# ReLU and row mean on one core: 127 rows a partition, the last 128 rows stored apart, and the tail shared between the engines

## The chip, the core and the metric

The kernel runs on one core of a Trainium2 chip. The metric is the device time of one execution in microseconds (us), the median of several runs. The profile is of one such execution; its span is some 1.8 us shorter than the measured time. Where two kernels are compared by a ratio, it is the mean time of one kernel's fast runs over that of the other's of the same rounds, so it is not quite the ratio of the medians that are quoted.

## The reference

```python
batch, seq, dim = 32, 512, 1024
x = np.random.randn(batch, seq, dim).astype(np.float32)      # 67.11 MB
relu_x = np.maximum(x, 0)
return np.mean(relu_x, axis=-1).astype(np.float32)           # 32 x 512 = 16,384 means, 65,536 B
```

Every number of x is read once and used once. The output is a thousandth of the input.

## The kernel before

The 16,384 rows are dealt to 128 partitions, 128 consecutive rows to each. A tile holds 16 rows of every partition (8 MB); seven full tiles come by one load each, the last one in pieces that get smaller, so that little work is left when the last byte lands. ScalarE and VectorE take the rows in turn; each makes the ReLU and the row's sum in one call (the trace shows it as two records, the pass over the row and a short read of the accumulated sum).

```python
    J = R // P                                               # 128 rows a partition
    xr = xf.rearrange("(p j) d -> p j d", p=P, j=J)
    outr = out.flatten().rearrange("(p j) -> p j", p=P, j=J)
    # ... seven tiles of 16 rows; the last tile in pieces of 8, 4, 2, 1 rows, its row 15 in 512, 256, 256 columns
    finish(0, j0)                                            # scale the sums of the first 112 rows
    # ... rows 0 to 13 of the last tile
    finish(j0, j0 + lo)

    last = xt[:, NB - 1, :]
    act_row(nc, xt[:, lo, :D // 2], part_a[:, 0:1])          # row 14, halved
    dve_row(nc, xt[:, lo, D // 2:], part_v[:, 0:1])
    act_row(nc, last[:, :D // 4], part_a[:, 1:2])            # row 15, four quarters
    dve_row(nc, last[:, D // 4:D // 2], part_v[:, 1:2])
    nc.vector.tensor_scalar(out=res[:, J - 2:J - 1], in0=part_a[:, 0:1], scalar1=part_v[:, 0:1], scalar2=inv,
                            op0=ALU.add, op1=ALU.mult)                                          # L106
    dve_row(nc, last[:, D // 2:3 * D // 4], part_v[:, 2:3])
    nc.vector.tensor_scalar(out=part_v[:, 1:2], in0=part_v[:, 1:2], scalar1=part_a[:, 1:2], scalar2=part_v[:, 2:3],
                            op0=ALU.add, op1=ALU.add)                                           # L111
    dve_row(nc, last[:, 3 * D // 4:], part_v[:, 3:4])
    nc.vector.tensor_scalar(out=res[:, J - 1:J], in0=part_v[:, 3:4], scalar1=part_v[:, 1:2], scalar2=inv,
                            op0=ALU.add, op1=ALU.mult)                                          # L116
    nc.sync.dma_start(out=outr, in_=res)                     # one store: 128 pieces of 512 B
```

## Time and profile before

| what | value | where it is read |
|---|---|---|
| time | 164.94 us (164.87 to 165.21, 4 runs) | runs |
| span of the profile | 163.1 us | page |
| last load landed | 159.19 us | landing records of the trace |
| last VectorE result | 160.61 us | timeline: 160.39 + 0.21 |
| store: issued, landed | 160.67, 162.22 us | timeline, landing records |

The page of the kernel before; the lines are the span, the busy time of the engines, the chain of work that ended last, and the store (KB, and us from issue to landing):

```profile
span 163.1 us, 351 instructions
DVE 75.4 (46%) x139; ACT 69.4 (43%) x133; POOL 0.2 (0%) x4
...
HBM read 67.11 MB, written 0.07 MB: 412 GB/s over the span
DMA 83%; DVE 14%; SPq 1%; issue 0%; DVEq 0%
...
out_dram<-res SPq DMA_DIRECT2D x1, 64.0 KB, 1.6
```

The kernel is bound by its loads: 83% of the chain is DMA, and the engines are busy less than half the time. Of the 896 packets of 65,536 B, the median took 2.418 us, which is 27.1 GB/s on each of 16 DMA engines, 434 GB/s in all. The Trainium skill ("DMA: Bandwidth & Descriptors", Specifications) gives the ceiling of the fabric as 435 GB/s, and the trace agrees. So a change can win only what lies after the last landing: 163.1 - 159.19 = 3.9 us.

The timeline of the kernel before, after the one-row piece has landed (start, us, engine, line, operation):

```profile
157.88 0.17 DVE L73 TENSOR_SCALAR res<-sum_v 128x7 f32<-128x7 f32 x1
...
157.96 0.68 DVE L20 TENSOR_SCALAR_CACHE_REDUCE xt<-xt 128x512 f32<-128x512 f32 x1
...
158.75 0.21 DVE L106 TENSOR_SCALAR res<-part_a,part_v 128x1 f32<-128x1 f32 x1
...
159.22 0.42 DVE L20 TENSOR_SCALAR_CACHE_REDUCE xt<-xt 128x256 f32<-128x256 f32 x1
159.56 0.08 DVE L20 DVE_READ_ACCUMULATOR xt<-xt 128x1 f32 x1
159.75 0.27 DVE L111 TENSOR_SCALAR part_v<-part_v,part_a 128x1 f32<-128x1 f32 x1
159.94 0.41 DVE L20 TENSOR_SCALAR_CACHE_REDUCE xt<-xt 128x256 f32<-128x256 f32 x1
160.27 0.08 DVE L20 DVE_READ_ACCUMULATOR xt<-xt 128x1 f32 x1
160.39 0.21 DVE L116 TENSOR_SCALAR res<-part_v 128x1 f32<-128x1 f32 x1
160.67 0.35 SPq L120 DMA_DIRECT2D out_dram<-res  x1
```

VectorE is late: the last 256 columns landed at 159.19 and their sum starts at 159.94. The small operations of lines 73, 106 and 111 are what made it late; those of lines 106 and 111 also wait some 0.1 us for the result just before them (159.56 + 0.08 to 159.75).

### The profile page before, as it was taken

What the parts mean: (1) busy time and instruction counts of PE and PEld (TensorE: products, weight loads), DVE (VectorE), ACT (ScalarE), POOL (GpSimd) and SP (SyncE); (2) the same over time, 40 slices, a digit from 0 to 9 for tenths busy, and PEclk for the clock granted to TensorE, in tenths of its full rate; (3) what the DMA queues carried; (4) which work ended last, traced back from release to release, by engine and by line L of the source; (5) the groups of instructions that cost most, each with busy time, mean ns of one, the idle gap of its engine ahead of it and who ended that gap; (6) DMA issues with size and microseconds to landing.
All of it is one profiled execution on the core that took longest, in us unless ns stands there. A gap on an engine that the chain in (4) does not pass through costs nothing.

```text
span 163.1 us, 351 instructions
## 1 busy us (share of the span) xinstructions
DVE 75.4 (46%) x139; ACT 69.4 (43%) x133; POOL 0.2 (0%) x4
## 2 busy tenths in 40 slices
DVE  0000039900596008940099202990059700799993
ACT  3000039700594008920099002980059500797890
POOL 0000000000000000000000000000000000000000
DMA  7979989989998998997997998998998897999970
GB/s 257 482 321 482 482 354 450 514 354 418 514 418 354 514 418 354 514 482 305 498 484 340 466 498 354 434 514 370 402 514 386 386 514 338 434 442 394 409 298 16
DMA packets 2162, 67.19 MB, mean 412 GB/s; under 512 B 240, under 2 KB 624, under 8 KB 880
## 3 DMA queue, kind: packets, MB, share of 16 engines
q1 hardware_dynamic: 2160, 67.18, 96.0%
q14 instruction: 2, 0.02, 0.0%
HBM read 67.11 MB, written 0.07 MB: 412 GB/s over the span
## 4 chain that ended last, share of the span: by engine, by line
DMA 83%; DVE 14%; SPq 1%; issue 0%; DVEq 0%
DMA xt<-in_x_dram 83%; DVE xt L20 13%; SPq L86 0%; SPq L79 0%; DVE part_v L111 0%; DVE res L116 0%; DVE res L106 0%; DVE res L73 0%; DVEq L20 0%; DVEq L111 0%; DVEq L106 0%
## 5 line engine op out<-in xcount | busy, mean ns | idle before, releaser
L20 DVE TENSOR_SCALAR_CACHE_REDUCE xt<-xt 128x1024 f32<-128x1024 f32 (+1 forms) x67 | 74.4, 1172 | 84.9 <-DMA xt<-in_x_dram 84.8
L15 ACT ACTIVATE xt<-xt 128x1024 f32<-128x1024 f32 (+1 forms) x65 | 66.7, 1027 | 88.9 <-DMA xt<-in_x_dram 88.9
L15 ACT ACTIVATION_READ_ACCUMULATOR xt<-xt 128x1 f32 x65 | 12.1, 187 | 0.0
L20 DVE DVE_READ_ACCUMULATOR xt<-xt 128x1 f32 x67 | 5.6, 83 | 0.0
L15 ACT ACT_TABLE_LOAD x1 | 1.3, 1283 | 0.7 <-PEq L135 0.7
L74 ACT ACTIVATE res<-sum_a 128x56 f32<-128x56 f32 (+1 forms) x2 | 0.5, 232 | 0.1
L73 DVE TENSOR_SCALAR res<-sum_v 128x56 f32<-128x56 f32 (+1 forms) x2 | 0.4, 184 | 0.1
L111 DVE TENSOR_SCALAR part_v<-part_v,part_a 128x1 f32<-128x1 f32 x1 | 0.3, 273 | 0.1
L106 DVE TENSOR_SCALAR res<-part_a,part_v 128x1 f32<-128x1 f32 x1 | 0.2, 214 | 0.1
L116 DVE TENSOR_SCALAR res<-part_v 128x1 f32<-128x1 f32 x1 | 0.2, 214 | 0.0
L135 POOL MEMSET const-uint8-127<- 128x1 uint8 x1 | 0.1, 102 | 0.0
L135 POOL MEMSET const-bfloat16-1.0<- 128x1 bf16 x1 | 0.1, 101 | 0.0
L135 POOL MEMSET const-float32-0.0<- 128x1 f32 x1 | 0.1, 98 | 0.2 <-issue 0.2
L135 POOL MEMSET const-float32-1.0<- 128x1 f32 x1 | 0.1, 98 | 0.0
## 6 DMA issues: line engine op xcount, KB each, us to landing
xt<-in_x_dram SPq DMA_DIRECT2D x1, 4096.0 KB, 39.0
xt<-in_x_dram SPq DMA_DIRECT2D x1, 2048.0 KB, 43.5
xt<-in_x_dram SPq DMA_DIRECT2D x1, 1024.0 KB, 45.5
xt<-in_x_dram SPq DMA_DIRECT2D x1, 512.0 KB, 46.3
xt<-in_x_dram SPq DMA_DIRECT2D x1, 256.0 KB, 46.5
xt<-in_x_dram SPq DMA_DIRECT2D x2, 128.0 KB, 42.7
xt<-in_x_dram SPq DMA_DIRECT2D x7, 48.9
out_dram<-res SPq DMA_DIRECT2D x1, 64.0 KB, 1.6
```

The lines of the kernel that those rows point to most:

```text
L15: nc.scalar.activation(out=src, in_=src, func=RELU, accum_out=acc)
L20: nc.vector.tensor_scalar(out=src, in0=src, scalar1=0.0, scalar2=None, op0=ALU.max, op1=ALU.add, accum_out=acc,)
L73: nc.vector.tensor_scalar_mul(out=res[:, lo + 1:hi:2], in0=sum_v[:, lo + 1:hi:2], scalar1=inv)
L74: nc.scalar.mul(out=res[:, lo:hi:2], in_=sum_a[:, lo:hi:2], mul=inv)
L106: nc.vector.tensor_scalar(out=res[:, J - 2:J - 1], in0=part_a[:, 0:1], scalar1=part_v[:, 0:1], scalar2=inv, op0=ALU.add, op1=ALU.mult,)
L111: nc.vector.tensor_scalar(out=part_v[:, 1:2], in0=part_v[:, 1:2], scalar1=part_a[:, 1:2], scalar2=part_v[:, 2:3], op0=ALU.add, op1=ALU.add,)
L116: nc.vector.tensor_scalar(out=res[:, J - 1:J], in0=part_v[:, 3:4], scalar1=part_v[:, 1:2], scalar2=inv, op0=ALU.add, op1=ALU.mult,)
L135: nc = _bacc.Bacc("TRN2", target_bir_lowering=False, num_devices=1)
```

## The change

Its intent: take the small operations off VectorE (GpSimd does the scaling), share the last row more evenly, and send nearly the whole output while the last row is still being summed. For that the last row of each partition must not lie between the others in memory, so each partition gets 127 rows, and the last 128 rows go one to a partition. What is left to store at the end is one value a partition, 128 x 4 B, side by side in memory.

```diff
-    xr = xf.rearrange("(p j) d -> p j d", p=P, j=J)
-    outr = out.flatten().rearrange("(p j) -> p j", p=P, j=J)
+    xr = xf[:P * (J - 1), :].rearrange("(p j) d -> p j d", p=P, j=J - 1)
+    outr = outf[:P * (J - 1)].rearrange("(p j) -> p j", p=P, j=J - 1)
+    xlast = xf[P * (J - 1):, :]
+    outlast = outf[P * (J - 1):].rearrange("(p o) -> p o", o=1)
 # ... finish(): one nc.gpsimd.tensor_scalar instead of one operation each on VectorE and ScalarE
+    act_row(nc, prev[:, :512], part[:, 0:1])
+    dve_row(nc, prev[:, 512:], part[:, 1:2])
+    nc.gpsimd.tensor_scalar(
+        out=res[:, J - 2:J - 1], in0=part[:, 0:1], scalar1=part[:, 1:2], scalar2=inv, op0=ALU.add, op1=ALU.mult,
+    )
+    nc.sync.dma_start(out=outr, in_=res[:, :J - 1])          # 128 pieces of 508 B, early
+    act_row(nc, last[:, :256], part[:, 2:3])
+    dve_row(nc, last[:, 256:512], part[:, 3:4])
+    nc.gpsimd.tensor_scalar(
+        out=part[:, 4:5], in0=part[:, 2:3], scalar1=inv, scalar2=0.0, op0=ALU.mult, op1=ALU.add,
+    )
+    act_row(nc, last[:, 512:640], part[:, 5:6])
+    dve_row(nc, last[:, 640:768], part[:, 6:7], init=part[:, 3:4])     # the sum starts from another
+    nc.scalar.activation(
+        out=part[:, 7:8], in_=part[:, 5:6], func=ACT.Identity, scale=inv, bias=part[:, 4:5],
+    )
+    dve_row(nc, last[:, 768:], part[:, 8:9], init=part[:, 6:7])
+    nc.vector.scalar_tensor_tensor(
+        out=end, in0=part[:, 8:9], scalar=inv, in1=part[:, 7:8], op0=ALU.mult, op1=ALU.add,
+    )
-    nc.sync.dma_start(out=outr, in_=res)
+    nc.sync.dma_start(out=outlast, in_=end)                  # 128 pieces of 4 B
```

The tail of before, shown above, goes. Called "after" from here on.

More of the change, by code (lines that the diff above doesn't have):

```diff
@@ L9, with dve_row @@
 ALU = mybir.AluOpType
-RELU = mybir.ActivationFunctionType.Relu
+ACT = mybir.ActivationFunctionType
 def act_row(nc, src, acc):
-    nc.scalar.activation(out=src, in_=src, func=RELU, accum_out=acc)
-def dve_row(nc, src, acc):
+    nc.scalar.activation(out=src, in_=src, func=ACT.Relu, accum_out=acc)
+def dve_row(nc, src, acc, init=None):
     nc.vector.tensor_scalar(
-        out=src, in0=src, scalar1=0.0, scalar2=None,
+        out=src, in0=src, scalar1=0.0, scalar2=init,
         op0=ALU.max, op1=ALU.add, accum_out=acc,
@@ L39 @@
     inv = 1.0 / D
-    xr = xf.rearrange("(p j) d -> p j d", p=P, j=J)
-    outr = out.flatten().rearrange("(p j) -> p j", p=P, j=J)
+    outf = out.flatten()
+    xr = xf[:P * (J - 1), :].rearrange("(p j) d -> p j d", p=P, j=J - 1)
+    outr = outf[:P * (J - 1)].rearrange("(p j) -> p j", p=P, j=J - 1)
+    xlast = xf[P * (J - 1):, :]
+    outlast = outf[P * (J - 1):].rearrange("(p o) -> p o", o=1)
     NB = 16
-    BUFS = 3
     full = J // NB - 1
-    row_pieces = []
-    left = NB
-    while left > 1:
-        row_pieces.append(left // 2)
-        left -= left // 2
-    col_pieces = [D // 2, D // 4, D // 4]
-    in_pool = ctx.enter_context(tc.tile_pool(name="in", bufs=BUFS))
+    row_pieces = [8, 4, 2, 1]
+    assert sum(row_pieces) == NB - 1
+    col_pieces = [512, 256, 256]
+    assert sum(col_pieces) == D
+    in_pool = ctx.enter_context(tc.tile_pool(name="in", bufs=3))
     res_pool = ctx.enter_context(tc.tile_pool(name="res", bufs=1))
-    sum_a = res_pool.tile([P, J], F32)
-    sum_v = res_pool.tile([P, J], F32)
+    sums = res_pool.tile([P, J], F32)
     res = res_pool.tile([P, J], F32)
-    part_a = res_pool.tile([P, 2], F32)
-    part_v = res_pool.tile([P, 4], F32)
+    part = res_pool.tile([P, 10], F32)
+    end = res_pool.tile([P, 1], F32)
     def rows(xt, lo, n, j0):
@@ L65, in rows @@
             j = j0 + k
-            if j % 2:
-                dve_row(nc, xt[:, k, :], sum_v[:, j:j + 1])
-            else:
-                act_row(nc, xt[:, k, :], sum_a[:, j:j + 1])
+            (dve_row if j % 2 else act_row)(nc, xt[:, k, :], sums[:, j:j + 1])
     def finish(lo, hi):
-        nc.vector.tensor_scalar_mul(out=res[:, lo + 1:hi:2], in0=sum_v[:, lo + 1:hi:2], scalar1=inv)
-        nc.scalar.mul(out=res[:, lo:hi:2], in_=sum_a[:, lo:hi:2], mul=inv)
+        nc.gpsimd.tensor_scalar(
+            out=res[:, lo:hi], in0=sums[:, lo:hi], scalar1=inv, scalar2=0.0, op0=ALU.mult, op1=ALU.add,
+        )
     for t in range(full):
@@ L83 @@
     xt = in_pool.tile([P, NB, D], F32, name="xt")
+    prev, last = xt[:, NB - 2, :], xt[:, NB - 1, :]
     lo = 0
@@ L89 @@
     for w in col_pieces:
-        nc.sync.dma_start(out=xt[:, lo, c:c + w], in_=xr[:, j0 + lo, c:c + w])
+        nc.sync.dma_start(out=last[:, c:c + w], in_=xlast[:, c:c + w])
         c += w
@@ L98 @@
     finish(j0, j0 + lo)
-    last = xt[:, NB - 1, :]
-    act_row(nc, xt[:, lo, :D // 2], part_a[:, 0:1])
-    dve_row(nc, xt[:, lo, D // 2:], part_v[:, 0:1])
-    act_row(nc, last[:, :D // 4], part_a[:, 1:2])
-    dve_row(nc, last[:, D // 4:D // 2], part_v[:, 1:2])
-    nc.vector.tensor_scalar(
-        out=res[:, J - 2:J - 1], in0=part_a[:, 0:1], scalar1=part_v[:, 0:1], scalar2=inv,
-        op0=ALU.add, op1=ALU.mult,
-    )
-    dve_row(nc, last[:, D // 2:3 * D // 4], part_v[:, 2:3])
-    nc.vector.tensor_scalar(
-        out=part_v[:, 1:2], in0=part_v[:, 1:2], scalar1=part_a[:, 1:2], scalar2=part_v[:, 2:3],
-        op0=ALU.add, op1=ALU.add,
-    )
-    dve_row(nc, last[:, 3 * D // 4:], part_v[:, 3:4])
-    nc.vector.tensor_scalar(
-        out=res[:, J - 1:J], in0=part_v[:, 3:4], scalar1=part_v[:, 1:2], scalar2=inv,
-        op0=ALU.add, op1=ALU.mult,
-    )
-    nc.sync.dma_start(out=outr, in_=res)
+    act_row(nc, prev[:, :512], part[:, 0:1])
+    dve_row(nc, prev[:, 512:], part[:, 1:2])
+    nc.gpsimd.tensor_scalar(
+        out=res[:, J - 2:J - 1], in0=part[:, 0:1], scalar1=part[:, 1:2], scalar2=inv, op0=ALU.add, op1=ALU.mult,
+    )
+    nc.sync.dma_start(out=outr, in_=res[:, :J - 1])
+    act_row(nc, last[:, :256], part[:, 2:3])
+    dve_row(nc, last[:, 256:512], part[:, 3:4])
+    nc.gpsimd.tensor_scalar(
+        out=part[:, 4:5], in0=part[:, 2:3], scalar1=inv, scalar2=0.0, op0=ALU.mult, op1=ALU.add,
+    )
+    act_row(nc, last[:, 512:640], part[:, 5:6])
+    dve_row(nc, last[:, 640:768], part[:, 6:7], init=part[:, 3:4])
+    nc.scalar.activation(
+        out=part[:, 7:8], in_=part[:, 5:6], func=ACT.Identity, scale=inv, bias=part[:, 4:5],
+    )
+    dve_row(nc, last[:, 768:], part[:, 8:9], init=part[:, 6:7])
[3 more added lines that the diff above has]
+    nc.sync.dma_start(out=outlast, in_=end)
 _INS = ['x']
```

## The prediction

> **What bounds the kernel now.** The load stream. The page's chain of work that ended last is 83% DMA, and the span is 163.1 us for 67.11 MB read. The packet records show 65,536 B packets at a constant 2.418 us from the second one on: 27.1 GB/s an engine, 434 GB/s on 16. The Trainium skill ("DMA: Bandwidth & Descriptors", Specifications) gives a fabric ceiling of 435 GB/s; this trace agrees, so the stream can't get faster. First packet 1.74 us, last load landing 159.19 us. VectorE needs 9.2 us for a tile of 16 rows against 19.4 us of transfer. Only what lies after the last landing, about 3.9 us of span, can be won.
>
> **The tail before (timeline of the last 8 us, and landings).** The one-row piece lands at 157.89, the column pieces at 158.53, 158.87 and 159.19. VectorE runs without a real gap from 156.62: two small scalings and joins (174, 214, 273 ns, each with about 0.1 us wait for its own previous result) stand between the row sums, so that the last 256 columns start at 159.94, 0.75 us after they landed. The last join ends at 160.61, the store is issued at 160.67, its first packet moves at 161.52, it lands at 162.22; closing barriers take the span to 163.1.
>
> **What the change does.**
> - Removes from VectorE the 174 ns scaling, the 214 and 273 ns joins and their waits, and 128 of 768 columns of the last row; about 0.9 us.
> - Adds: two sums that start from the previous one's result, so each waits for it (about 0.12 us) and reads a pointer operand (about 60 ns by 214 against 174 and 273 ns). About 0.35 us back, all on the chain. My chain: half row 157.9 to 158.55, 256 columns to 158.97, 128 to 159.4, 256 to 160.0, final join 160.15 to 160.4.
> - GpSimd has no arithmetic in the trace of before, so its op time is unknown. The join of partials before ScalarE's closing op must finish by about 159.8. [...] At 1 us an op it becomes the chain, and the end comes at about 161.2.
> - The large store (64 KB, 1.6 us) goes out near 159.2 to 159.6, hidden. The final store is 512 B as 128 pieces of 4 B. The 64 KB store needed 0.85 us to its first packet, 0.35 us of packets, 0.35 us to land; I expect 0.1 to 0.2 us saved.
> - Row pitch a partition goes from 512 to 508 KiB. The Trainium skill (same page, "Latency and other measured facts") has power-of-two pitches slowing copies, at 512 KiB by 3%. This trace shows 512 KiB already at the ceiling, so I expect nothing, at most 0.3 us in the first packets (2.7 to 3.5 us against 2.418).
>
> **Sum.** Final join 0.2 us earlier, store 0.1 us shorter: span about 162.8, time 164.6 us. A tail of no cost would gain little over 2%, so "within 2%".
>
> **Right if:** 65,536 B packets stay at 2.418 us; last landing within 0.2 us of 159.19; last VectorE result at 160.2 to 160.6; final store lands 1.3 to 1.6 us after issue; no VectorE or ScalarE wait on GpSimd over 0.3 us.
>
> **Wrong if:** GpSimd ops take about 1 us (time near 165.4); stores of 4 B or of 508 B at unaligned addresses land much later than 1.6 us (up to 1 us lost); the new pitch disturbs the stream (1% is 1.6 us), or speeds its first packets.

## The result, and the profile after

The changed kernel takes 169.97 us (169.65 to 170.03, 4 runs) against 164.94 us: ratio 1.0298, 95% interval 1.028 to 1.0316. It is slower by 5 us, outside the range predicted.

The page of after: the span, the busy time of the engines and the chain of work that ended last:

```profile
span 167.9 us, 360 instructions
DVE 74.8 (45%) x135; ACT 69.6 (41%) x134; POOL 1.2 (1%) x8
...
DMA 81%; DVE 12%; SPq 1%; issue 0%; DVEq 0%
```

The stores, with KB and us from issue to landing, from the DMA view of after:

```profile
out_dram<-res SPq DMA_DIRECT2D x1, 63.5 KB, 1.8
out_dram<-end SPq DMA_DIRECT2D x1, 0.5 KB, 7.2
```

512 B took 7.2 us where 64 KB had taken 1.6. The timeline of after shows that everything before it went well:

```profile
158.40 0.27 POOL L102 TENSOR_SCALAR res<-part 128x1 f32<-128x1 f32 x1 [0.55 <-ACT xt L15]
...
158.68 0.35 DVE L20 TENSOR_SCALAR_CACHE_REDUCE xt<-xt,part 128x128 f32<-128x128 f32 x1
158.69 0.35 SPq L105 DMA_DIRECT2D out_dram<-res  x1
158.81 0.19 POOL L108 TENSOR_SCALAR part<-part 128x1 f32<-128x1 f32 x1
...
159.07 0.48 DVE L20 TENSOR_SCALAR_CACHE_REDUCE xt<-xt,part 128x256 f32<-128x256 f32 x1
159.11 0.29 ACT L113 ACTIVATE part<-part 128x1 f32<-128x1 f32 x1
...
159.67 0.16 DVE L117 SCALAR_TENSOR_TENSOR end<-part 128x1 f32<-128x1 f32 x1
159.86 0.34 SPq L120 DMA_DIRECT2D out_dram<-end  x1
```

The last load landed at 158.82 and the last result was there at 159.83, 0.78 us earlier than before. The last store was issued at 159.86 and landed at 167.03. In sum: the issue comes 0.81 us earlier, the store takes 7.17 - 1.55 = 5.62 us longer, together +4.81 us; the spans differ by 4.8 us. The waits of SyncE, whose last wait is for the stores (us in total, times, longest), first before, then after:

```profile
SPq L146 <- DMA out_dram<-res: 1.0, 1, 1.0
```
```profile
SPq L146 <- DMA out_dram<-end: 6.5, 1, 6.5
```

The chain view hides this: it follows the engines' work, and that ended at 159.83. Where the waiting lies within the store is in the packet and landing records: the last of the 4 B packets had been taken up by a DMA engine at 160.89, but the 16 engines reported their landings one after another, from 162.65 to 167.03. By these records it is the confirmation of the writes that takes long, not the engines' own packets.

### The profile page after: what moved, and what is told of

Read it like the earlier page. It is cut to its first block, busy times and chain, and to the rows that moved or that the text cites. A ratio compares the mean times of both kernels' runs of the same rounds, so it can differ in the third digit from the quotient of the medians.

```text
span 167.9 us, 360 instructions
## 1 busy us (share of the span) xinstructions
DVE 74.8 (45%) x135; ACT 69.6 (41%) x134; POOL 1.2 (1%) x8
## 4 chain that ended last, share of the span: by engine, by line
DMA 81%; DVE 12%; SPq 1%; issue 0%; DVEq 0%
DMA xt<-in_x_dram 81%; DVE xt L20 12%; SPq L84 1%; SPq L76 0%; DVE end L117 0%; DVEq L20 0%; DVEq L117 0%
## 5 line engine op out<-in xcount | busy, mean ns | idle before, releaser
L69 POOL TENSOR_SCALAR res<-sums 128x112 f32<-128x112 f32 (+1 forms) x2 | 0.5, 254 | 156.9 <-DVE xt L20 156.9
L20 DVE TENSOR_SCALAR_CACHE_REDUCE xt<-xt,part 128x128 f32<-128x128 f32 (+1 forms) x2 | 0.8, 412 | 0.1
```

What stands on the lines that cost most here:

```text
L20: nc.vector.tensor_scalar(out=src, in0=src, scalar1=0.0, scalar2=init, op0=ALU.max, op1=ALU.add, accum_out=acc,)
L69: nc.gpsimd.tensor_scalar(out=res[:, lo:hi], in0=sums[:, lo:hi], scalar1=inv, scalar2=0.0, op0=ALU.mult, op1=ALU.add,)
```

## The experiments

The landing times below are from the landing records, to two places; the fences show the DMA view's rounded ones. For each kernel the edit is against after, unless it says otherwise. Kernels that leave part of the output unwritten, or write it in the wrong place, do so on purpose.

### Is it the last store at all?

`one_store` has after's tail and GpSimd work, with the layout and the one store of before:

```diff
-    xr = xf[:P * (J - 1), :].rearrange("(p j) d -> p j d", p=P, j=J - 1)   # and outr, xlast, outlast
+    xr = xf.rearrange("(p j) d -> p j d", p=P, j=J)                        # outr likewise
+    xlast = xr[:, J - 1, :]
-    nc.sync.dma_start(out=outr, in_=res[:, :J - 1])
-    nc.sync.dma_start(out=outlast, in_=end)
+    nc.sync.dma_start(out=outr, in_=res)       # the last join writes to res[:, J - 1:J] in place of end
```

> After's tail and GpSimd scaling, but 128 rows a partition and one 64 KB store of 512 B pieces, as before. Theory (the store of 128 pieces of 4 B is the whole loss, 7.17 us from issue to landing against 1.55 us): the store lands 1.5 to 1.6 us after its issue, the last join ends 0.3 to 0.8 us earlier than before's 160.61, time 164.1 to 164.6 us. Rival (the 508 KiB row pitch, GpSimd or the new tail cost time): 165 us or more. Last load landing near 159.2 if the pitch is what made after's 158.8; near 158.8 if it was chance.

Measured: 164.69 us (6 runs; before 165.00 in the same rounds), ratio 0.9976 (0.9953 to 0.9999), correct. The store landed 1.55 us after its issue. The last result came 0.98 us after the last landing, against 1.42 in before. The time lies just above the range written. The loss is gone with the layout and the second store, so neither the new tail nor GpSimd is the cause.

`col_512` keeps both stores, but has 128 rows a partition, so that the 128 pieces of 4 B lie 512 B apart:

```diff
+    # layout as in one_store
-    nc.sync.dma_start(out=outr, in_=res[:, :J - 1])
+    nc.sync.dma_start(out=outr[:, :J - 1], in_=res[:, :J - 1])
-    nc.sync.dma_start(out=outlast, in_=end)
+    nc.sync.dma_start(out=outr[:, J - 1:J], in_=end)
```

> Two stores as in after, and still 128 pieces of 4 B last, but with 128 rows a partition, so that the pieces lie 512 B apart in memory instead of side by side. Theory A (writes of under a small block of memory that fall in the same block are done one after another): the small store lands in 1.3 to 2.0 us, time 164.0 to 165.0. Theory B (each 4 B piece is slow in itself, wherever it goes; 8 to an engine): again 7 us, time near 170.

Measured: 164.39 us (4 runs; before 165.00), ratio 0.9966 (0.9931 to 1.0001), correct. The same number of 4 B pieces lands in 1.41 us:

```profile
out_dram<-end SPq DMA_DIRECT2D x1, 0.5 KB, 1.4
```

So a 4 B piece is not slow in itself (theory B falls). What is slow is that they lie side by side (theory A). The Trainium skill ("DMA: Bandwidth & Descriptors", Specifications) says that below 512 B a DMA engine reads, modifies and writes; whether it does so here no run shows, but by itself the size costs nothing visible in this store.

`small_alone` leaves the first store out, to see whether the second one waits for it:

```diff
-    nc.sync.dma_start(out=outr, in_=res[:, :J - 1])
```

> After without its 63.5 KB store (most of the output is not written, wrong on purpose); only the store of 128 pieces of 4 B side by side is left. Theory A and B: it still lands about 7 us after its issue. Theory C (it waits for the unaligned 508 B pieces stored just before it): under 2 us.

Measured: 7.68 us from issue to landing (one look). The first store has no part in it (theory C falls).

`fix_127` keeps after's layout and both stores, and turns the last results so that they go out as 4 pieces of 128 B to the same 512 B:

```diff
-    outlast = outf[P * (J - 1):].rearrange("(p o) -> p o", o=1)
+    outlast = outf[P * (J - 1):].rearrange("(b c) -> b c", c=32)
-    end = res_pool.tile([P, 1], F32)
+    end = res_pool.tile([P, 32], F32)          # zeroed early; the results go to its first column
+    turned = res_pool.tile([P, 32], F32)
-    nc.sync.dma_start(out=outlast, in_=end)
+    nc.vector.transpose(out=turned, in_=end)   # 32 x 32 blocks
+    nc.sync.dma_start(out=outlast, in_=turned[0:P:32, :])
```

> After with one thing changed: the last 128 results are turned on VectorE from a column of 128 partitions into 4 rows of 32, and the last store writes 4 pieces of 128 B to the same 512 B. If the many 4 B pieces side by side are the whole loss: the store lands 1.3 to 1.6 us after issue, the turn costs 0.2 to 0.4 us, time 164.1 to 164.6 us. If the place (these 512 B, just after the first store's) or the second store itself were slow: over 168 us.

Measured: 164.50 us (5 runs; before 165.10), ratio 0.9965 (0.9953 to 0.9978), correct. The turn took 0.21 us, the store landed 1.62 us after its issue (the last of its landing records; the DMA view gives no time for it). This is the change with its one fault mended: 5.5 us faster than after as first measured (169.97; not in the same rounds).

### Why are neighbouring 4 B pieces slow?

Two theories were left: an engine's own neighbouring pieces wait for each other (E), or pieces of several engines in the same few bytes do (F). The first set changes the number of pieces or their pitch.

```diff
 # first16, first32, first64: only the first n of the 128 values are stored
+    nc.sync.dma_start(out=outlast[:16, :], in_=end[:16, :])
 # pitch64B, pitch16B, pitch8B (n = 16, 4, 2): all 128, into a part of the output that the first store leaves out
+    nc.sync.dma_start(out=outr[:112, :], in_=res[:112, :J - 1])
+    apart = outf[14336:14336 + n * P].rearrange("(p s) -> p s", s=n)
+    nc.sync.dma_start(out=apart[:, :1], in_=end)
```

> After, but only 16 partitions of the last column are stored, 16 pieces of 4 B side by side (64 B), one piece to a DMA engine; the other 112 values are not written, wrong on purpose. Theory A with a block of 64 B (16 writes queue for one block, and the eight blocks of after were written side by side): still 6 to 7 us. Theory A with one queue for all 128 writes (about 0.05 us a piece): 2 to 2.3 us. Theory B (8 slow pieces to an engine, now 1): about 2 us.

> The last store writes its 128 pieces of 4 B at a pitch of 64 B instead of 4 B (into a part of the output that the first store now leaves out; wrong values on purpose). At 512 B pitch they landed 1.41 us after issue, side by side 7.17 us. Theory A1 (pieces collide only within 64 B): 1.4 us. Theory A2 (within 512 B, here 8 pieces to a block): between 1.6 and 3 us.

> The same with a pitch of 16 B: 4 pieces to 64 B, and if an engine takes 4 neighbouring partitions, these 4 come from one engine. Theory E (pieces of one engine collide, each waiting for the one before): still 6 to 7 us. Theory F (it is the number of pieces, or of engines, in one block that costs): 1.4 to 3 us.

> 32 pieces of 4 B side by side, two to an engine (16 pieces, one to an engine, landed in 1.38 us; 128 pieces, eight to an engine, in 7.17 us). Theory E (a queue of an engine's own neighbouring pieces): a step at two pieces, 2.0 to 2.5 us. Theory F (one queue for all pieces of a block of 512 B, cost by the number of pieces, about 0.05 us each): 1.4 to 2.5 us. If it stays at 1.4 us the cost starts only with more pieces.

> 64 pieces of 4 B side by side, four to an engine. Theory E: 3.3 to 4.5 us (about 0.75 us for each further piece of an engine). Theory F: 3 to 4 us if the cost is by the piece, under 2.5 us if it grows faster than the number of pieces.

> 128 pieces of 4 B at a pitch of 8 B (wrong values on purpose). At 16 B, four pieces to 64 B, they landed in 1.42 us, side by side in 7.17 us. If pieces collide when more than four fall in 64 B: between 3 and 7 us. If they collide only when they touch or share 8 B: 1.4 us.

Measured, from issue to landing: first16 1.38 us, first32 3.31, first64 7.11; pitch64B 1.61, pitch16B 1.42, pitch8B 2.79. Every range written for first32 and first64 was missed, first16 came in below all of its own, and pitch8B fell just under the range of the theory that fits it: neither E nor F as written gave the numbers of first32 and first64. A time by the piece alone is out: first64 is as slow as all 128. So is a block of 64 B: first16 fills one and is fast, and first32 has no more pieces to 64 B and is slow. In first32 half of the engines reported late, in steps of 0.43 us (161.49, 161.92, 162.35, 162.78, 163.22): a queue.

`first17` and `apart_64` test E directly, `pieces16B` asks whether touching matters:

```diff
 # first17
+    nc.sync.dma_start(out=outlast[:17, :], in_=end[:17, :])
 # apart_64: pieces that follow one another in the copy go 64 B apart, within the same 512 B
+    spread = outf[P * (J - 1):].rearrange("(b a o) -> a b o", b=8, o=1)
+    nc.sync.dma_start(out=spread, in_=end)
 # pieces16B: end is 4 values wide, 128 pieces of 16 B side by side, to the place of pitch16B
+    nc.sync.dma_start(out=apart, in_=end)
```

> 17 pieces of 4 B side by side. 16 is not a divisor of 17, and by the Trainium skill (DMA: Bandwidth & Descriptors, section on why a DMA increments its semaphore by 16) such a copy runs on one DMA engine; then no other engine writes near it. Theory E (an engine's own neighbouring pieces wait for each other, about 0.4 us each as the steps in first32's landings): over 6 us. Theory F (it takes several engines that write into the same 64 B at once, more than one piece each): 1.3 to 1.7 us.

> The same 512 B as in after, 128 pieces of 4 B from 128 partitions on 16 engines, but in another order: the pieces that follow one another go 64 B apart, so neighbouring addresses are written by different engines, and each 64 B gets pieces from all engines (values in the wrong places on purpose). Theory E: 1.3 to 1.7 us. Theory F (pieces of several engines in one 64 B, many at once): 5 us or more.

> 128 pieces of 16 B side by side, 2 KB (values are filler, wrong on purpose): four pieces to 64 B, as with 4 B pieces at a pitch of 16 B (1.42 us) but without holes. Under both theories, if what counts is the number of pieces in 64 B (four or fewer are free): 1.3 to 1.7 us. If it is pieces that touch: 3 us or more. 64 B pieces side by side took 1.42 us.

Measured: first17 1.26 us, apart_64 7.21, pieces16B 1.42. Theory E falls: 17 neighbouring pieces of one engine land at once. That it was one engine is what the Trainium skill ("DMA: Bandwidth & Descriptors", section on why a DMA increments its semaphore by 16) gives for 17 partitions, which have no other divisor up to 16 than 1, and the records agree: besides one update at 160.38, soon after the issue, a single landing came, at 161.20. apart_64 is as slow as after, in another order of the pieces. (It passed the check of the output although its values were meant to be out of place. By a calculation on inputs of this kind, not a run, the permutation changes the output by only some 0.5% in the root mean square; that the check can't tell so little is inferred, and that the order changed rests on the access pattern alone.) 16 B pieces that touch are as fast as 4 B pieces with holes.

### A count in 256 B

All these runs agree with one count, made after the fact: how many pieces, from several engines, fall in one aligned block of 256 B, counted from the start of the output (theory G). 16 to a block (first16, pitch16B, pieces16B): about 1.4 us. 32 (first32, pitch8B): 2.8 to 3.3. 64 (first64, after, apart_64, small_alone): 7.1 to 7.7, and 128 pieces are no slower than 64, because they are two blocks. So it was tested on runs for which it makes a number in advance:

```diff
 # shift64: first64, moved by 128 B
+    nc.sync.dma_start(out=outlast[32:96, :], in_=end[:64, :])
 # shift32: first32, moved by 192 B
+    nc.sync.dma_start(out=outlast[48:80, :], in_=end[:32, :])
 # first48
+    nc.sync.dma_start(out=outlast[:48, :], in_=end[:48, :])
```

> first64 with the address moved by 128 B and nothing else: the same 64 pieces side by side from the same 64 partitions, but the first 32 now end an aligned 256 B and the last 32 begin the next one (values in the wrong places on purpose). Theory G, made from the runs so far: what counts is the number of pieces from several engines in one aligned block of 256 B, 16 free and some 0.12 us for each further one; 32 to a block as in first32 and pitch8B, so 2.8 to 3.5 us instead of first64's 7.1. If it is the number of pieces in all, or the block is 512 B or more: again about 7 us.

> first32 moved by 192 B: 16 of its pieces end one aligned 256 B and 16 begin the next. Theory G: 1.3 to 1.6 us, as first16 and pitch16B. If the number of pieces in all counts, or 64 or 128 B blocks do: 3.3 us as first32.

> 48 pieces of 4 B side by side in one aligned 256 B, three to an engine. Theory G with 0.12 us for each piece over 16: 1.4 + 32 x 0.12 = 5.2 us (4.5 to 5.9). If the cost were a step between 32 and 64 pieces: about 3.3 or about 7.1.

Measured: shift64 3.50 us, shift32 1.35, first48 5.30. The DMA view of first64 and then of shift64:

```profile
out_dram<-end SPq DMA_DIRECT2D x1, 0.2 KB, 7.1
```
```profile
out_dram<-end SPq DMA_DIRECT2D x1, 0.2 KB, 3.5
```

And of first32 and then of shift32:

```profile
out_dram<-end SPq DMA_DIRECT2D x1, 0.1 KB, 3.3
```
```profile
out_dram<-end SPq DMA_DIRECT2D x1, 0.1 KB, 1.4
```

And of first16 and then of first48:

```profile
out_dram<-end SPq DMA_DIRECT2D x1, 0.1 KB, 1.4
```
```profile
out_dram<-end SPq DMA_DIRECT2D x1, 0.2 KB, 5.3
```

The same pieces from the same partitions, moved in memory by half a block, take half as long; and 48 pieces fit the slope: (5.30 - 1.38) / 32 = 0.12 us for each piece above 16, as (3.31 - 1.38) / 16 and (7.11 - 1.38) / 48 do. Runs with the same count are not equal, though: with 32 to a block they took 2.79 (pitch8B), 3.31 and 3.50 us, which is 0.09 to 0.13 us for each piece above 16. The expectation of shift32 errs in one point: blocks of 128 B would have given a short time too, since the move leaves 16 pieces in each of two such blocks. It is first48 and first64 that rule out 128 B, for with it no block would hold more than 32 pieces and both would take first32's 3.31; and shift64, which lies within one block of 512 B, rules out 512.

What in the memory system makes the queue, and where between 16 and 32 pieces it begins, stays open. The words "from several engines" are not shown either: the one run with a single engine, first17, has only 17 pieces, for which the count alone gives about 1.5 us, so that it excludes theory E but not a queue of one engine's many pieces. Nor do the packet records name the engine, so how many engines share a block, and whether their number matters, is open.

### A version that beats both

`gather_one` has the layout and the one store of before, GpSimd's scaling, and another tail: each column piece is halved between the two engines, no sum starts from another, and one short sum over the six partial sums ends it. `gather_tiled` has the same tail with each tile contiguous in memory, the results of seven tiles stored early, and 128 pieces of 64 B, four to 256 B, at the end.

```diff
 # both: the tail of after from last[:, :256] on is replaced
+    c = 0
+    for i, w in enumerate(col_pieces):
+        act_row(nc, last[:, c:c + w // 2], part[:, 2 + 2 * i:3 + 2 * i])
+        dve_row(nc, last[:, c + w // 2:c + w], part[:, 3 + 2 * i:4 + 2 * i])
+        c += w
+    nc.vector.tensor_scalar(
+        out=junk, in0=part[:, 2:8], scalar1=inv, scalar2=None,
+        op0=ALU.mult, op1=ALU.add, accum_out=res[:, J - 1:J],
+    )
 # gather_one
+    nc.sync.dma_start(out=outr, in_=res)
 # gather_tiled; the loads take xt_all[t]
+    xt_all = xf.rearrange("(t p k) d -> t p k d", t=T, p=P, k=16)
+    outr = outf.rearrange("(t p k) -> p t k", t=T, p=P, k=16)
+    nc.sync.dma_start(out=outr[:, :full, :], in_=res[:, :j0].rearrange("p (t k) -> p t k", k=16))   # after finish(0, j0)
+    nc.sync.dma_start(out=outr[:, full, :], in_=res[:, j0:])                                        # at the end
```

> 128 rows a partition and one store of 512 B pieces as before; GpSimd scaling as after; each column piece of the last row is halved between ScalarE and VectorE, no sum starts from another, and one short VectorE sum over the six partial sums ends it. one_store ended its join 0.98 us after the last landing, before 1.42 us. Here 0.6 to 0.75 us, store 1.55 us, time 164.1 to 164.5 us.

> As gather_one, but each tile of 16 rows a partition is one contiguous 8 MB block (row pitch a partition 64 KiB), the results of the first seven tiles are stored early, and the last store writes 128 pieces of 64 B side by side. If the layout with 508 KiB pitch landed its last load 0.3 us earlier because 512 KiB is a bad pitch, 64 KiB may land early too (158.9) or late (159.4). If only pieces far under 64 B collide, the last store lands in 1.3 to 1.6 us: time 163.8 to 164.4. If 64 B pieces side by side collide too: over 167.

Measured in the same rounds: gather_one 164.16 us (5 runs), ratio to before 0.9945 (0.9933 to 0.9958); gather_tiled 163.99 us (5 runs), ratio 0.9937 (0.9923 to 0.995); before 165.10. Both are correct. The gain of about 0.6% is small, but the intervals lie clear of 1. The end of gather_tiled's timeline:

```profile
159.24 0.29 DVE L20 TENSOR_SCALAR_CACHE_REDUCE xt<-xt 128x128 f32<-128x128 f32 x1
...
159.51 0.19 ACT L15 ACTIVATION_READ_ACCUMULATOR xt<-xt 128x1 f32 x1
159.73 0.16 DVE L111 TENSOR_SCALAR_CACHE_REDUCE junk<-part 128x6 f32<-128x6 f32 x1 [0.20 <-ACT xt L15]
159.81 0.08 DVE L111 DVE_READ_ACCUMULATOR junk<-part 128x1 f32 x1
159.96 0.35 SPq L115 DMA_DIRECT2D out_dram<-res  x1
```

The last load landed at 159.21, and VectorE starts on it at once (159.24). The result is there 0.68 us after that landing, against 1.01 in after and 1.42 in before. The sum of 128 columns takes 0.28 to 0.29 us here and 0.35 in after, where it starts from another sum; that start also made it wait. The last store landed in 1.42 us, against 1.54 for the 64 KB of gather_one.

## Why the prediction was wrong

**The bound: right.** Packets of 65,536 B have a median of 2.418 us in after too. The loads still set the pace, and only the tail could change.

**The last store: the step that failed.** The prediction said: "I expect 0.1 to 0.2 us saved". It took 7.17 us in place of 1.55, 5.62 us lost. The sum of first packet, packets and landing was carried over from pieces of 512 B to pieces of 4 B, on the argument that the transfer is smaller. The term that failed is the landing: from the end of the last packet of the store it took 0.35 us in before and 0.37 in col_512, but 6.13 in after (160.90 to 167.03). The size was looked at and the address was not: 64 pieces fell into each 256 B. The list of what could go wrong did name 4 B stores, with "up to 1 us lost"; that bound had no measurement behind it and was over five times too small.

**The tail: right in kind, its gain undersized.** Predicted was a last result 0.2 us earlier, with a window of 160.2 to 160.6; it came 0.78 us earlier, at 159.83. Of this, 159.185 - 158.824 = 0.36 us is an earlier last landing, and 1.422 - 1.006 = 0.42 us is a shorter way from there. one_store, with the same tail on before's layout, gives the second part again (0.98).

**The row pitch: "at most 0.3 us", about right.** The last load landed at 158.82 to 159.16 (mean 159.00) in the 15 profiles with 127 rows a partition, and at 159.19 to 159.39 (mean 159.29) in the 4 with 128 rows. It is not the steady rate, which is the same; it arises at the start. The first 16 packets had all ended by 5.39 to 5.76 us with 127 rows and by 5.81 to 5.91 with 128, and the first tile had landed at 22.82 and 23.13 us in the mean, so the whole difference is there by then. (gather_tiled, with a pitch of 64 KiB, landed its first tile earliest of all, at 22.59, and its last load at 159.21 all the same: an early start alone does not settle it.) No run changed the pitch alone and the profiles are from several chips, so that 508 KiB is a better pitch than 512 is argued, not shown. The prediction asked for a landing within 0.2 us of 159.19, and the one of after missed that.

**GpSimd: right.** Its operations in the tail took 0.27 and 0.19 us, far from the 1 us at which the prediction saw them become the chain. The Trainium skill ("Perfetto Trace Analysis", on GPSIMD instructions) calls such spans unreliable, but what waited for them agrees: SyncE issued the first store at 158.69, just after 158.40 + 0.27, and ScalarE's closing operation started at 159.11, after 158.81 + 0.19. No engine of the chain waited for it.

**The first store: hidden, as predicted.** It landed at 160.50, far ahead of the end. Its unaligned 508 B pieces needed 1.81 us, which nothing waited for.

## What to carry to other kernels

Before you split a small result off into a store of its own, ask where its pieces land: 4 B from each of 128 partitions, side by side, took 7.2 us here, and with 16 B between their starts, or as a few pieces of 128 B, 1.4 to 1.6 us. Read a store's time from issue to landing and not only the chain of engine work, for an engine chain that ends earlier says nothing about when the last write is confirmed. An estimate for a transfer is carried over from another one only if the size of the pieces and their addresses are alike.

## What the Trainium skill lacked or had wrong

- "DMA: Bandwidth & Descriptors": nothing there tells that many small writes into the same 256 B of memory queue up. Runs: 16 pieces of 4 B in an aligned 256 B land in 1.38 us, 32 in 3.31, 48 in 5.30, 64 in 7.11, some 0.12 us for each above 16 (one look each); moved by half a block, the 64 land in 3.50. The section on how a descriptor splits into AXI transactions has blocks of 256 B, but says nothing of this.
- The same page, Specifications: the minimum of 512 B for full rate leads one to fear small pieces as such. 128 pieces of 4 B at a pitch of 512 B landed in 1.41 us, 128 of 16 B side by side in 1.42, and 128 of 512 B in 1.55. These are times of one small store and not rates, so they add to that figure and do not contradict it.
- The same page, on the row pitch: slowing at a pitch of 512 KiB, measured there on copies between HBM tensors, is not seen in these loads to the core's own memory; packets took 2.418 us at 512 and at 508 KiB.
- "GPSIMD Engine Reference": I found no time for a small operation. By the profile, operations on 128x1 to 128x112 took 0.19 to 0.29 us.
- The pages on VectorE ("VectorE: DVE Perf Modes" and "DVE: scalar operands, raw-bit mode, write accounting and state across instructions", both under Scalar operands): I found no time for a pointer operand, that is a column of a tile in place of a constant. A sum of 128 columns that starts from another sum took 347 ns, without it 281 to 286 ns, so some 60 ns more, and about 0.1 us of waiting for the other result.
